# Weight columns of a dense expert pass: row one-hot times gate on ScalarE, column one-hot on VectorE in 32 bits, the PSUM copy one step later, and no products on GpSimd

## The chip, the cores and the metric

The kernel runs on one core of one Trainium2 chip. The time is the device time of one launch in microseconds (us); lower is better. Before the change it is 3195.77 us, the median of 3 runs (3186.97 to 3201.72).

## The reference, cut to what matters

An encoder block on 1024 tokens of width 1024: a mixer (attention and a short convolution, both gated), then PEER, an expert layer that this change touches. PEER chooses 16 of 128 x 128 single-neuron experts per token and head, 8 heads:

```python
q = (xc @ w_query).reshape(c, PEER_HEADS, 2, PEER_HALF_DIM)
sc = jnp.einsum('chpd,hpnd->chpn', q, sub_keys)
s1, i1 = lax.top_k(sc[:, :, 0], PEER_TOPK)
s2, i2 = lax.top_k(sc[:, :, 1], PEER_TOPK)
cand = (s1[..., :, None] + s2[..., None, :]).reshape(c, PEER_HEADS, -1)
top, pos = lax.top_k(cand, PEER_TOPK)
eidx = jnp.take_along_axis(cidx, pos, axis=-1)      # cidx = i1 * 128 + i2
g = jax.nn.softmax(top, axis=-1)
a = jax.nn.gelu(jnp.einsum('chkd,cd->chk', expert_u[eidx], xc))
out = jnp.einsum('chk,chkd->cd', g * a, expert_v[eidx])
```

## The kernel before, in words

The 1024 tokens are 8 tiles of 128. Tiles 0 to 4 (group 0) get a dense expert pass: all 16384 experts are multiplied, and a weight that is zero for experts not chosen is multiplied in. Tiles 5 to 7 (group 1) gather the rows of their chosen experts from HBM, two VectorE passes a row (L746, L755).

The stages, in the order of time: projections and mixer of group 0, its expert scores (`scores`, L556; `pq`, `pcs`), then the mixer and the scores of group 1 (lines `pc`, `px`, `pb`, `pg`, `ps`, `po`, `py`, `ph`, `pq`), then the dense pass (`z`, `pout`, `held` on TensorE, L905) with the gather of group 1 beside it, and the rest of the gather.

Two jobs run beside the scores of group 0 and the mixer of group 1. `select_gen` (L594) chooses the experts of a tile in two halves of 4 heads: top 16 of 128 by max, find and replace (L588 to L592), the same among candidates, then by one-hots the indices: `sc<-pf,iota_k` on VectorE (L637), times the index on GpSimd (L639), summed on VectorE (L640). `weights_gen` (L686) turns the chosen indices of a dense tile into columns of weights: 4 tokens (`WQ`) a step, 8 steps a block of 32 (`WT`), 4 blocks a tile, 5 tiles: 160 steps. In a step VectorE makes both one-hots in 16 bits in one instruction (`ms`, L714, 1024 elements), GpSimd multiplies the row one-hot by the gate (`o1`, L718), ScalarE copies the column one-hot into 32 bits (`o2`, L720), TensorE multiplies the two for each token (`pw`, L695), and ScalarE copies the result into `wbuf` (L696), which goes to HBM by block (`w_d`, L726). `o1` and `o2` lie token by token, so that an instruction which writes them for 4 tokens at once, token innermost, steps 512 bytes from each element to the next. `ms`, `o1` and `o2` have two buffers each, `wbuf` one.

The dense pass reads the columns back (`wt<-w_d`, L920) and multiplies them in on VectorE (`pr`, L930) ahead of the split `ph`, `phl` (L896, L898) that the second half of the dense products needs.

The jobs are generators that `tick` advances by modelled time of TensorE. Then a scheduler sets each engine's order by its own model of time; on the chip each engine goes through its own list in that order and waits where an operand is late. After the last mixer line, `drain(wgt)` (L881) runs what is left of the columns.

Of the kernel before, what the change touches and what calls it, by code (L numbers as in the profile page):

```python
# [10 lines left out]
F32 = mybir.dt.float32  # L11
BF16 = mybir.dt.bfloat16
# [3 lines left out]
AF = mybir.ActivationFunctionType  # L16
ALU = mybir.AluOpType
# [3 lines left out]
P = 128  # L21
# [29 lines left out]
WT = 32  # L51
WQ = 4
# [13 lines left out]
def block_kernel(ctx, tc, x, wqkv, wcols, wpr, wo, wq, skT, uv, uT, an_w, fn_w, fin_w, sub_w,  # L66
# [527 lines left out]
    def select_gen(small, tt, ev, gw, done=None):  # L594
# [6 lines left out]
        for a in range(2):  # L601
# [5 lines left out]
                top16(t, sc[:, hp, :], NK, sv[:, hp, :], si[:, hp, :])  # L607
                yield
            ohs = sc.rearrange("p h c -> p (h c)").bitcast(BF16).rearrange("p (j h a k) -> p j h a k", j=2, a=TOPK, k=TOPK)
            sf = t([P, PH, TOPK], F32, "sf")  # L610
            V.tensor_copy(out=sf, in_=si)
            svv = sv.rearrange("p (h q) k -> p h q k", q=2)
            sfv = sf.rearrange("p (h q) k -> p h q k", q=2)
# [11 lines left out]
            for j in range(2):  # L625
                pi, pj, pf = t(s3, U32, "pi"), t(s3, U32, "pj"), t(s3, BF16, "pf")
                if j == 0:
                    V.tensor_scalar(pi, ti, 4, None, op0=ALU.logical_shift_right)
                    V.tensor_scalar(pj, ti, 2, None, op0=ALU.logical_shift_right)
                    V.scalar_tensor_tensor(pf, pj, -12.0, pi, op0=ALU.add, op1=ALU.max)  # L630
                else:
                    V.tensor_scalar(pi, ti, 12, None, op0=ALU.bitwise_and)
                    V.tensor_scalar(pj, ti, 3, None, op0=ALU.bitwise_and)
                    V.scalar_tensor_tensor(pf, ti, 64.0, pi, op0=ALU.is_lt, op1=ALU.mult)
                    V.tensor_tensor(out=pf, in0=pf, in1=pj, op=ALU.add)
                oh = ohs[:, j]
                V.tensor_tensor(out=oh, in0=pf.unsqueeze(2).broadcast_to(sh), in1=iota_k.unsqueeze(1).broadcast_to(sh),  # L637
                                op=ALU.is_equal)
                PL.tensor_tensor(out=oh, in0=oh, in1=sfv[:, :, j, :].unsqueeze(3).broadcast_to(sh), op=ALU.mult)  # L639
                V.tensor_reduce(out=ev[j][:, a * 64:(a + 1) * 64].rearrange("p (h k) -> p h k", k=TOPK),  # L640
                                in_=oh.rearrange("p h a k -> p h k a"), axis=AX.X, op=ALU.add)
                yield
# [41 lines left out]
        yield from select_gen(t, tt, ev, gw, done)  # L684

    def weights_gen(wf):  # L686
        later = []
# [3 lines left out]
        def finish(buf, q, o1, o2):  # L691
            for t in range(0, WQ, 4):
                pw = ps["w"].tile([P, 4, NK], F32, name="pw", tag="g")
                for u in range(4):
                    PE.matmul(pw[:, u, :], lhsT=o2[:, t + u, :], rhs=o1[:, t + u, :], start=True, stop=True)  # L695
                A.copy(out=buf[:, :, q + t:q + t + 4], in_=pw.rearrange("p t i -> p i t"))  # L696

        for c in range(NB):
            while c >= len(chosen):
                yield  # L700
            pt = ps["w"].tile([P, 4, P], F32, name="ptw", tag="g")
            for j, s in enumerate(chosen[c]):
                PE.transpose(out=pt[:, j, :], in_=s, identity=ident)
            ib = wf.tile([P, 2, P], BF16, name="ib", tag="ib", bufs=2)
            A.copy(out=ib, in_=pt[:, 0:2, :])
            w = wf.tile([P, P], F32, name="wtr", tag="wtr", bufs=2)
            A.copy(out=w, in_=pt[:, 2, :])
            for b in range(P // WT):
# [116 lines left out]
    with ExitStack() as pb:  # L825
# [7 lines left out]
        with ExitStack() as st:  # L833
# [209 lines left out]
```

## Time and profile before

| | us |
|---|---|
| median of 3 runs | 3195.77 |
| the profiled execution, its own time | 3191.78 |
| span of its instructions | 3190.0 |
| busy TensorE, VectorE, ScalarE, GpSimd | 3012.1, 2646.3, 1302.9, 923.5 |
| columns: first and last `ms` starts | 732.6, 1313.4 |
| first and last product of the dense pass | 1317.7, 3147 |

Some 1.8 us of the execution lie outside the span. Busy shares of the whole span mix stages with different limits; the rows further below are therefore by stretch of time. In the stretch of the columns TensorE, VectorE, ScalarE and GpSimd all take part, and the stage ends when the last column has gone to HBM and come back.

### The profile page before, as it was taken

The page shows a single profiled execution, that of the slowest core. Times are in us where ns is not written, and L with a number is a line of the kernel's source. Part 1 is how long each engine was busy: PE and PEld are TensorE (multiplying, and loading weights), DVE is VectorE, ACT ScalarE, POOL GpSimd, SP SyncE. Part 2 cuts the span into 40 slices and gives each one's busy share as a digit, 9 for nine tenths or more (in the row PEclk, how much of TensorE's full clock was granted, in tenths as well). Part 3 has the DMA queues.
Part 4 walks back from the last instruction along what each step waited for, and adds up shares of the span by engine and source line. Part 5 has one row for each costly group of instructions (what it writes and reads, how often), then busy time and mean ns, then how long its engine had stood idle before and what let it go on. Part 6 is the DMA issues. An engine that isn't in the chain of part 4 may idle for free.

```text
span 3190.0 us, 45907 instructions
## 1 busy us (share of the span) xinstructions
PE 3012.1 (94%) x17551; PEld 2761.0 (87%) x17551; DVE 2646.3 (83%) x4665; ACT 1302.9 (41%) x2344; POOL 923.5 (29%) x716
## 2 busy tenths in 40 slices
PE   7999999898989879799999999999999999999994
PEld 6799998798988869789989989899889999999993
DVE  5442466378999996799999999999999999999898
ACT  3322364335567766533333333333333333333332
POOL 2310000035344444223222222223332323333333
PEclk9999999999999989899999999999999999999997
DMA  5451232555444375779878888888889999898887
GB/s 180 145 182 67 83 113 80 199 172 213 146 172 157 144 260 196 255 249 333 316 277 321 316 299 309 295 316 293 313 328 343 340 341 348 326 347 325 328 336 281
DMA packets 237549, 801.11 MB, mean 251 GB/s; under 512 B 18832, under 2 KB 123280, under 8 KB 174096
## 3 DMA queue, kind: packets, MB, share of 16 engines
q0 software_dynamic: 64704, 442.53, 37.5%
q1 hardware_dynamic: 152592, 305.30, 27.8%
q10 hardware_dynamic: 20032, 50.34, 4.1%
q8 instruction: 138, 2.26, 0.3%
q14 instruction: 83, 0.68, 0.1%
HBM read 714.74 MB, written 83.36 MB: 250 GB/s over the span
## 4 chain that ended last, share of the span: by engine, by line
PE 56%; DVE 17%; issue 11%; DMA 8%; POOL 4%; ACT 3%; SPq 0%; ACTq 0%; POOLq 0%; DVEq 0%
PE z L905 17%; PE pout L905 10%; PE held L905 6%; PE pq L228 4%; PE pg L228 4%; POOL uvt L739 3%; PE ph L228 3%; DMA uvt<-in_uv,idx 3%; DVE acc L755 2%; PE py L228 2%; PE pw L695 2%; DVE uvt L746 2%; DVE ms L714 1%; PE pv L228 1%; PE pk L228 1%
## 5 line engine op out<-in xcount | busy, mean ns | idle before, releaser
L739 POOL DMA_INDIRECT uvt<-in_uv,idx x384 | 528.1, 1375 | 1288.5 <-DVE acc L755 1011.0
L905 PE MATMUL z<-actTh,uh 128*128 128x320 f32 x2048 | 636.3, 311 | 5.5 <-ACT pr L929 4.5
L905 PE MATMUL z<-actTh,uhl 128*128 128x320 f32 x2048 | 636.5, 311 | 1.1 <-DVE uhl L898 1.1
L905 PE MATMUL z<-actTl,uh 128*128 128x320 f32 x2048 | 635.3, 310 | 0.0
L746 DVE SCALAR_TENSOR_TENSOR uvt<-uvt,hng 128x1024 f32<-128x1024 f32 x384 | 468.0, 1220 | 41.1 <-DMA uvt<-in_uv,idx 40.3
L755 DVE SCALAR_TENSOR_TENSOR acc<-uvt,wt,acc 128x1024 f32<-128x1024 f32 x381 | 487.8, 1280 | 1.3 <-ACT wt L749 1.2
L905 PEld LDWEIGHTS z<-actTh,uh 128*128 128x128 f32 x2048 | 386.0, 188 | 20.5 <-ACT pr L929 8.6
L905 PEld LDWEIGHTS z<-actTl,uh 128*128 128x128 f32 x2048 | 386.2, 189 | 10.1
L905 PEld LDWEIGHTS z<-actTh,uhl 128*128 128x128 f32 x2048 | 386.8, 189 | 8.5 <-DVE uhl L898 2.2
L905 PE MATMUL pout<-vh,ph 128*128 128x512 f32 x768 | 302.5, 394 | 23.2 <-ACT ph L896 15.0
L905 PE MATMUL pout<-vhl,ph 128*128 128x512 f32 x768 | 301.1, 393 | 0.0
L905 PE MATMUL pout<-vh,phl 128*128 128x512 f32 x768 | 300.5, 391 | 0.0
L718 POOL TENSOR_TENSOR o<-ms,wtr 128x512 f32<-128x512 bf16 x160 | 203.0, 1311 | 262.1 <-PE pw L695 123.4
L748 ACT ACTIVATE wt<-zt 128x1 f32<-128x1 f32 x384 | 77.0, 201 | 493.3 <-DVE uvt L746 493.0
L957 DVE TENSOR_TENSOR hacc<-pout,hacc 128x512 f32<-128x512 f32 x384 | 259.4, 681 | 19.6 <-PE pout L905 19.1
L185 DVE TENSOR_TENSOR wl<-wr,wh 128x2048 fp32r<-128x2048 f32 x66 | 157.9, 2392 | 117.7 <-ACT wh L184 117.7
L896 ACT CAST uh<-raw 128x1024 fp32r<-128x1024 f32 x128 | 134.3, 1049 | 193.5 <-DMA raw<-in_uT 187.9
L184 ACT CAST wh<-wr 128x2048 fp32r<-128x2048 f32 x74 | 141.0, 1907 | 168.9 <-DMA wr<-in_wq 31.6
L695 PE MATMUL pw<-o,o 128*128 128x128 f32 x1280 | 169.1, 284 | 41.2 <-POOL o L718 17.6
L695 PEld LDWEIGHTS pw<-o,o 128*128 128x128 f32 x1280 | 161.1, 198 | 49.3 <-issue 25.6
L905 PE MATMUL held<-vhl,ph 128*128 128x512 f32 x512 | 199.6, 391 | 0.0
L720 ACT CAST o<-ms 128x512 f32<-128x512 bf16 x160 | 179.6, 1138 | 38.8 <-DVE ms L714 26.0
(290 smaller groups left out, 6673.5 us busy)
## 6 DMA issues: line engine op xcount, KB each, us to landing
raw<-in_uT SPq DMA_DIRECT2D x128, 512.0 KB
raw<-in_uv SPq DMA_DIRECT2D x128, 512.0 KB
w_d<-wbuf ACTq DMA_DIRECT2D x20, 2048.0 KB
wt<-w_d SPq DMA_DIRECT2D x32, 1280.0 KB
wr<-in_wcols SPq DMA_DIRECT2D x28, 1024.0 KB
wr<-in_wq SPq DMA_DIRECT2D x24, 1024.0 KB
xt<-in_x SPq DMA_DIRECT2D x16, 512.0 KB
q_d<-qt POOLq DMA_DIRECT2D x32, 256.0 KB
```

The lines of the kernel that those rows point to most:

```text
L184: A.copy(out=op[0][sl], in_=src)
L185: lo.tensor_sub(op[1][sl], src, op[0][sl].bitcast(F32))
L228: PE.matmul(pd, lhsT=l[a], rhs=r[b], start=i == 0 and j == 0, stop=i == n - 1 and j == len(c) - 1)
L695: PE.matmul(pw[:, u, :], lhsT=o2[:, t + u, :], rhs=o1[:, t + u, :], start=True, stop=True)
L718: PL.tensor_tensor(out=o1.rearrange("p t i -> p i t"), in0=ms[:, 0], in1=w[:, ts].unsqueeze(1).broadcast_to(sh), op=ALU.mult)
L720: A.copy(out=o2.rearrange("p t i -> p i t"), in_=ms[:, 1])
L739: PL.indirect_dma_start(out=t[:], out_offset=None, in_=uv, in_offset=bass.IndirectOffsetOnAxis(ap=sels[c][1][:, k:k + 1], axis=0))
L746: V.scalar_tensor_tensor(u, u, 1.0, st[c], op0=ALU.mult, op1=ALU.mult, accum_out=zt)
L755: V.scalar_tensor_tensor(st["acc"], v, wt, st["acc"], op0=ALU.mult, op1=ALU.add)
L896: A.copy(out=hi, in_=t)
L905: PE.matmul(ps, lhsT=lhs[k][a], rhs=rhs[k][b], start=first and k == 0 and j == 0, stop=last and k == n - 1 and j == 2)
L957: V.tensor_add(hacc[:, t - NR, ds], ps, hacc[:, t - NR, ds])
```

## The change

The one-hot instruction of a step makes the row one-hot alone, in 16 bits (512 elements). A second VectorE instruction makes the column one-hot straight into the 32-bit `o2`, by the strided write. ScalarE makes `o1` with four instructions, one a token, each a copy scaled by the gate. The copy out of PSUM (`keep`) comes a step after its products (`columns`), and blocks and tiles are no longer drained where they end, but once at the end (`flush`), and once before the PSUM pool of the first stretch closes. In the selection the product with the index moves from GpSimd to VectorE, and the indices `sf` are kept in 16 bits.

```diff
-            sf = t([P, PH, TOPK], F32, "sf")
+            sf = t([P, PH, TOPK], BF16, "sf")
...
-                PL.tensor_tensor(out=oh, in0=oh, in1=sfv[:, :, j, :].unsqueeze(3).broadcast_to(sh), op=ALU.mult)
+                V.tensor_tensor(out=oh, in0=oh, in1=sfv[:, :, j, :].unsqueeze(3).broadcast_to(sh), op=ALU.mult)
...
+        def operands(c, b, q, ib, w):
+            ts = slice(b * WT + q, b * WT + q + WQ)
+            ms = wf.tile(sh, BF16, name="ms", tag="ms")
+            V.tensor_tensor(out=ms, in0=ib[:, 0, ts].unsqueeze(1).broadcast_to(sh), in1=iota_t, op=ALU.is_equal)
+            o2 = wf.tile([P, WQ, NK], F32, name="o2", tag="o2")
+            V.tensor_tensor(out=o2.rearrange("p t i -> p i t"), in0=ib[:, 1, ts].unsqueeze(1).broadcast_to(sh),
+                            in1=iota_t, op=ALU.is_equal)
+            o1 = wf.tile([P, WQ, NK], F32, name="o1", tag="o1")
+            for u in range(WQ):
+                A.activation(o1[:, u, :], ms[:, :, u], AF.Copy, scale=w[:, b * WT + q + u:b * WT + q + u + 1])
+            made.append((c, b, q, o1, o2))
...
                 for q in range(0, WT, WQ):
-                    ms = wf.tile([P, 2] + sh[1:], BF16, name="ms", tag="ms")
-                    V.tensor_tensor(out=ms, in0=ib[:, :, ts].unsqueeze(2).broadcast_to([P, 2] + sh[1:]),
-                                    in1=iota_t.unsqueeze(1).broadcast_to([P, 2] + sh[1:]), op=ALU.is_equal)
...
-                    PL.tensor_tensor(out=o1.rearrange("p t i -> p i t"), in0=ms[:, 0],
-                                     in1=w[:, ts].unsqueeze(1).broadcast_to(sh), op=ALU.mult)
-                    A.copy(out=o2.rearrange("p t i -> p i t"), in_=ms[:, 1])
-                    if later:
-                        finish(*later.pop(0))
-                    later.append((buf, q, o1, o2))
+                    operands(c, b, q, ib, w)
+                    if done:
+                        keep()
+                    if len(made) > 1:
+                        columns()
                     yield
-                finish(*later.pop(0))
-                A.dma_start(out=w_d[c * (P // WT) + b], in_=buf)
+            flush()
```

The scheduler then puts the work in other places. First TensorE, where the scores of group 1 end and the dense pass begins (`pq`, `pcs` are the scores, `pw` one step of columns, `z` the dense pass), before:

```order
L228 MATMUL pq_12064<-hnTh,wl 128x384
L695 MATMUL pw<-o_10523,o_10524 128x128 x4
L564 MATMUL pcs<-sk,qp 128x128 x3
L695 MATMUL pw<-o_10535,o_10536 128x128 x4
L564 MATMUL pcs<-sk,qp 128x128 x3
L695 MATMUL pw<-o_10547,o_10548 128x128 x4
L695 MATMUL pw<-o_10559,o_10560 128x128 x4
L905 MATMUL z<-actTh,uh 128x320
```

And the same place now:

```order
L228 MATMUL pq_12578<-hnTh,wl 128x384
L564 MATMUL pcs<-sk,qp 128x128 x6
L708 MATMUL pw<-o_10670,o_10668 128x128 x4
L708 MATMUL pw<-o_10720,o_10718 128x128 x4
...
L708 MATMUL pw<-o_11022,o_11020 128x128 x4
L708 MATMUL pw<-o_11037,o_11035 128x128 x4
L925 MATMUL z<-actTh,uh 128x320
```

Two steps of columns stood between the last score and the dense pass; now there are 14. Second VectorE, from the last one-hots to the first `pr` of the dense pass (`sv`, `si`, `tk` are the second half of tile 5's selection, `e` its sums, `idx` the indices of its first half), before:

```order
L714 TENSOR_TENSOR ms<-ib,iota_t 128x1024
L679 SCALAR_TENSOR_TENSOR idx<-e_12215,e_12216 128x64
L898 TENSOR_TENSOR uhl<-raw,uh 128x1024 x2
L898 TENSOR_TENSOR vhl<-raw,vh 128x1024 x2
L588 MAX sv<-sc 128x8 x6
L589 MAX_INDEX si<-sv,sc 128x8
...
L592 MAX_INDEX si<-sv,tk_12591 128x8
L930 TENSOR_TENSOR pr<-pr,wt 128x640
L590 MATCH_REPLACE tk_12597<-sv,sc 128x128
L591 MAX sv<-tk_12597 128x8
```

And now:

```order
L918 TENSOR_TENSOR vhl<-raw,vh 128x1024
L697 TENSOR_TENSOR o_10864<-ib,iota_t 128x128x4
L695 TENSOR_TENSOR ms<-ib,iota_t 128x512
...
L590 MATCH_REPLACE tk_13183<-sv,sc 128x128
L697 TENSOR_TENSOR o_11035<-ib,iota_t 128x128x4
L591 MAX sv<-tk_13183 128x8
...
L639 TENSOR_TENSOR sc<-sc,sf 128x1024
L640 TENSOR_REDUCE e_12696<-sc 128x64
L950 TENSOR_TENSOR pr<-pr,wt 128x640
```

The whole second half of tile 5's selection now stands ahead of the first `pr`, most of it ahead of the last one-hot of the columns (`o_11035`), together with five of the splits `uhl` and `vhl`.

## Rows read from the trace of the kernel before

**Rows 1.** Windows: stretch, length; busy of PE, PEld, DVE, ACT, POOL; clock; DMA; GB/s.

```profile
0.00:695.20 695.20, 655.03 (x3978) 599.57 (x3979) 338.13 (x550) 260.65 (x439) 90.26 (x112) 0.98 0.40 137
695.20:1224.10 528.90, 465.74 (x2950) 440.61 (x2950) 492.71 (x1327) 338.22 (x497) 237.64 (x172) 0.95 0.50 182
1224.10:1317.20 93.10, 91.89 (x643) 91.34 (x641) 61.02 (x149) 66.33 (x95) 39.10 (x31) 1.00 0.47 165
1317.20:1360.30 43.10, 25.25 (x144) 23.49 (x145) 24.62 (x91) 12.51 (x15) 5.76 (x5) 0.80 0.98 342
1360.30:3147.00 1786.70, 1772.73 (x9837) 1605.14 (x9836) 1697.73 (x2512) 616.18 (x1274) 536.68 (x386) 1.00 0.88 318
3147.00:3190.00 43.00, 1.46 (x7) 0.85 (x5) 32.08 (x42) 9.00 (x26) 14.08 (x12) 0.57 0.72 266
```

**Rows 2.** Waits of VectorE from 695.2 to 1224.1: total us, times, longest.

```profile
DVE sv L588 <- DMA sc<-sc_d: 9.7, 4, 5.6
DVE ms L714 <- ACT o L720: 7.3, 4, 2.9
DVE wl L185 <- ACT wh L184: 7.1, 5, 2.5
DVE ms L714 <- POOL o L718: 3.0, 3, 1.0
```

**Rows 3.** Chain of waits at the stage's end: start, length, work.

```profile
1317.69 10.34 DMA w_d<-wbuf
1328.05 19.98 DMA wt<-w_d
1348.06 0.83 DVE pr L930
```

**Rows 4.** A step's instructions: min/median/max ns; then groups: busy us, mean ns.

```profile
L714 DVE TENSOR_TENSOR ms<-ib,iota_t x160: 654/679/2030, 732.6 to 1313.4; 128x1024 bf16<-128x1024 bf16 x160
L718 POOL TENSOR_TENSOR o<-ms,wtr x160: 1056/1132/3630, 733.4 to 1314.2; 128x512 f32<-128x512 bf16 x160
L720 ACT CAST o<-ms x160: 1058/1133/1367, 733.3 to 1314.2; 128x512 f32<-128x512 bf16 x160
L696 ACT COPY wbuf<-pw x160: 563/592/765, 738.4 to 1317.0; 128x512 f32<-128x512 f32 x160
...
L714 DVE TENSOR_TENSOR ms<-ib,iota_t 128x1024 bf16<-128x1024 bf16 x160 | 128.6, 816 | 32.3 <-ACT o L720 22.6 <-POOL o L718 9.7
```

**Rows 5.** VectorE elsewhere: dense 512, strided and dense reductions of 1024; ns.

```profile
L957 DVE TENSOR_TENSOR hacc<-pout,hacc x384: 660/682/699, 1365.0 to 3153.6; 128x512 f32<-128x512 f32 x192
L640 DVE TENSOR_REDUCE e<-sc x32: 2003/2123/2265, 684.8 to 2274.4; 128x64 f32<-128x1024 bf16 x32
L387 DVE TENSOR_REDUCE nm<-ps x64: 1197/1216/1226, 354.6 to 1074.6; 128x1 f32<-128x1024 f32 x64
```

**Rows 6.** Two `ms` in a row in the chain of waits.

```profile
822.17 1.21 DVE ms L714 x2
```

**Rows 7.** Stretched VectorE instructions: min/median/max ns, and means by group.

```profile
L634 DVE SCALAR_TENSOR_TENSOR pf<-ti,pi x16: 207/460/1934, 682.0 to 2255.1; 128x64 bf16<-128x64 uint32 x16
...
L634 DVE SCALAR_TENSOR_TENSOR pf<-ti,pi 128x64 bf16<-128x64 uint32 x16 | 15.0, 940 | 0.0
...
L185 DVE TENSOR_TENSOR wl<-wr,wh x66: 2268/2291/3779, 11.4 to 1287.6; 128x2048 fp32r<-128x2048 f32 x66
...
L185 DVE TENSOR_TENSOR wl<-wr,wh 128x2048 fp32r<-128x2048 f32 x30 | 75.5, 2516 | 12.0 <-ACT wh L184 12.0
```

**Rows 8.** ScalarE, a copy of 128 elements with a per-partition scale.

```profile
L449 ACT ACTIVATE at<-po,rz x32: 349/367/493, 371.8 to 1103.3; 128x128 f32<-128x128 f32 x32
```

**Rows 9.** Waits of TensorE from 695.2 to 1317.2, those of the columns.

```profile
PE pw L695 <- POOL o L718: 17.6, 15, 3.0
PE pw L695 <- ACT o L720: 12.6, 10, 4.2
PE pw L695 <- ACT wbuf L696: 10.9, 3, 9.2
```

More of the change, by code (lines that the diff above doesn't have):

```diff
@@ L686, in weights_gen, with columns, keep, flush @@
     def weights_gen(wf):
-        later = []
         iota_t = wf.tile([P, NK, WQ], BF16, name="iota_t", tag="iota_t", bufs=1)
         repeated_iota(wf, iota_t, "wtr")
[L691 to L696, printed above, removed]
+        made, done, at = [], [], {}
+        sh = [P, NK, WQ]
+        def operands(c, b, q, ib, w):
[9 more added lines that the diff above has]
+            made.append((c, b, q, o1, o2))
+        def columns():
+            c, b, q, o1, o2 = made.pop(0)
+            pw = ps["w"].tile([P, WQ, NK], F32, name="pw", tag="g")
+            for u in range(WQ):
+                PE.matmul(pw[:, u, :], lhsT=o2[:, u, :], rhs=o1[:, u, :], start=True, stop=True)
+            done.append((c, b, q, pw))
+        def keep():
+            c, b, q, pw = done.pop(0)
+            if q == 0:
+                at["buf"] = wf.tile([P, NK, WT], F32, name="wbuf", tag="wbuf", bufs=1)
+            A.copy(out=at["buf"][:, :, q:q + WQ], in_=pw.rearrange("p t i -> p i t"))
+            if q == WT - WQ:
+                A.dma_start(out=w_d[c * (P // WT) + b], in_=at["buf"])
+        def flush():
+            while done:
+                keep()
+            while made:
+                columns()
+                keep()
+        state["flush"] = flush
         for c in range(NB):
@@ L708, in weights_gen @@
             for b in range(P // WT):
-                buf = wf.tile([P, NK, WT], F32, name="wbuf", tag="wbuf", bufs=1)
                 for q in range(0, WT, WQ):
-                    ts = slice(b * WT + q, b * WT + q + WQ)
-                    sh = [P, NK, WQ]
-                    ms = wf.tile([P, 2] + sh[1:], BF16, name="ms", tag="ms")
-                    V.tensor_tensor(out=ms, in0=ib[:, :, ts].unsqueeze(2).broadcast_to([P, 2] + sh[1:]),
-                                    in1=iota_t.unsqueeze(1).broadcast_to([P, 2] + sh[1:]), op=ALU.is_equal)
-                    o1 = wf.tile([P, WQ, NK], F32, name="o1", tag="o1")
-                    o2 = wf.tile([P, WQ, NK], F32, name="o2", tag="o2")
-                    PL.tensor_tensor(out=o1.rearrange("p t i -> p i t"), in0=ms[:, 0],
-                                     in1=w[:, ts].unsqueeze(1).broadcast_to(sh), op=ALU.mult)
-                    A.copy(out=o2.rearrange("p t i -> p i t"), in_=ms[:, 1])
-                    if later:
-                        finish(*later.pop(0))
-                    later.append((buf, q, o1, o2))
+                    operands(c, b, q, ib, w)
+                    if done:
+                        keep()
+                    if len(made) > 1:
+                        columns()
                     yield
-                finish(*later.pop(0))
-                A.dma_start(out=w_d[c * (P // WT) + b], in_=buf)
+            flush()
     def gather_gen(gat):
@@ L854, in block_kernel @@
             ready.update(range(2, NB))
+            state["flush"]()
     pa = ExitStack()
```

## The prediction, made before the changed kernel was run

> **What bounds the kernel now.** I read the windows by stage first, since the change sits in one stage. In [rows 1] the columns run from the second to the third stretch, 695.2 to 1317.2 us. In the second, VectorE is busy 492.7 of 528.9 us (93%), TensorE 465.7 (88%), ScalarE 64%, GpSimd 45%. In the third, which holds the scores of group 1, TensorE is busy 91.9 of 93.1 us and VectorE only 61.0. So VectorE sets the pace until 1224 and TensorE from there to 1317. The fourth stretch is a wait: the last block of columns goes out in 10.3 us and comes back in 20.0 us before `pr` can start [rows 3]. The dense pass that follows is TensorE's (1772.7 of 1786.7 us busy), and the last 43 us are the rest of the gather. The dense pass cannot absorb a late start: what the column stage ends later moves the end by nearly as much.
>
> Second I read the waits of VectorE in the second stretch [rows 2]. Of 36.2 us idle (528.9 - 492.7), 16.8 are waits for operands from memory or for a split (9.7 + 7.1), which stay; 10.3 are waits of `ms` for ScalarE and GpSimd to free a buffer (7.3 + 3.0). Third, the durations of a step's instructions [rows 4].
>
> **The change part by part.** All on VectorE unless said; paces are durations less the overlap with the next instruction. Two `ms` of 679 ns median took 1.21 us together [rows 4, 6], so the pace is 0.60 us, 0.07 to 0.08 below the duration.
>
> `ms` halved. 1024 elements take 654 ns at least; with about 0.12 us fixed (an estimate), half of the rest is 0.27, so 0.39 in duration and 0.33 in pace. Bounds are half the old pace, 0.30, and three quarters of it, 0.45. Saved: 160 x (0.60 - 0.33) = 43 us (24 to 48).
>
> `o2`, new. No row shows VectorE writing single 32-bit elements 512 bytes apart. From below it costs as a dense instruction of 512: 682 ns [rows 5], pace 0.61. ScalarE does this same write now, and takes 1133 ns for 512 elements where its unstrided write of 512 takes 592 [rows 4]: 0.54 us for the stride. VectorE's own nearest row is a reduction that reads single elements apart, 2123 ns for 1024 against 1216 for the dense one [rows 5]: 0.91 for 1024, 0.45 for 512. Added to 682 that is 1.13 to 1.22 us. The nearest row by kind of access is ScalarE's write, whose whole instruction takes 1133 ns with a larger fixed part. I take 1.07 us, a little under it, thus a pace of 1.0, and keep 0.61 below and 1.30 above (twice the dense row, as the stride makes ScalarE's 1.9 times its own). Added: 160 x 1.0 = 160 us (98 to 208).
>
> ScalarE's row shows that the stride costs, in this memory and at this step. [...]
>
> Products of the selection. Up to the first `pr` the 12 halves of tiles 0 to 5 are chosen, two products each: 24. [...] Added: 24 x 1.15 = 28 us (14 to 29). On GpSimd they vanish, and it waits for nothing that ends late.
>
> Stretching that ends. `ms` has a mean of 816 ns and a median of 679 [rows 4]: 160 x 0.137 = 22 us. `pf` has a mean of 940 and a least of 207 [rows 7]: 16 x 0.73 = 12. `wl` has a mean of 2516 here and a median of 2291 over the run: 30 x 0.225 = 7. These 41 us are instructions that take up to three or nine times their least while GpSimd works (237.6 + 39.1 us in both stretches, [rows 1]); almost all of GpSimd's work goes. Smaller groups do the same, so I take 60 us (41 to 80). [...]
>
> The order. The second half of tile 5's selection and five splits now stand ahead of the last `o2`, or soon behind it. Before, they were most of VectorE's 24.6 us (91 instructions) between 1317 and 1360 and some after it [rows 1]. Three quarters of that, 18 us (10 to 25), now delay the last column. What remains behind the last `o2` lies under the 30 us in which the columns go out and back [rows 3], and costs nothing; without that cover it would be some 15 us.
>
> Net on VectorE up to the last column: 160 - 43 + 28 - 60 + 18 = 103 us more.
>
> What it can use up: its idle time in the third stretch, 93.1 - 61.0 = 32 us, and 8 of the 10 us in which `ms` waited for a buffer: 40 us. The stage therefore ends 103 - 40 = 63 us later.
>
> TensorE has the same instructions. Its 14 steps in a row wait for VectorE, and that wait is the 63 us seen from the other side. ScalarE trades 160 x 1.13 = 181 us for 640 copies at about 0.37 [rows 8], 235 us: 54 more, and even with 0.1 more each for the strided read 118; it has 622 - 404.5 = 217 us free in the two stretches [rows 1], so this is hidden. In the last 14 steps, a step costs it 4 x 0.37 + 0.59 = 2.1 us, 29 us in all; VectorE needs 14 x 1.33 and the 18 us moved there, 37 us, so there too ScalarE is the lesser. The copy out of PSUM a step later frees ScalarE from waits and moves nothing. The indices in 16 bits cost nothing.
>
> In the dense pass VectorE loses the moved selection (some 20 us) and gains 8 products (9 us); TensorE's idle time there is 14 us in all [rows 1], so I put the gain at 5 us (0 to 10). The gather's tail stays.
>
> Sum, on the profiled execution's 3191.8 us: 3191.8 + 63 - 5 = 3250 us. That execution is 4 us under the median of 3195.8, which is within the spread of the three runs; so I predict 3250, 1.7% slower.
>
> **The rivals.**
>
> The strided write costs more: a pace of 1.30. The sum rises by 160 x 0.30 = 48 to 3298 us. For it: ScalarE's instruction nearly doubles by the stride. Against: the strided read adds less.
>
> The strided write is as cheap as a dense one, pace 0.61: 62 us less, net 41, which the 40 us of idle time take up. Then 3191.8 - 5 = 3187 us, no change that can be told. For it: no VectorE row shows a penalty on a write. Against: the same write on ScalarE.
>
> The other side: the hand-offs decide, not VectorE's load. TensorE waits 17.6 + 12.6 + 10.9 = 41 us for the columns' GpSimd product, ScalarE copy and PSUM copy [rows 9]; the new pipeline has no GpSimd in it and copies late. If VectorE's net stays under its 40 us of idle time, which needs `o2` at a pace of 0.60, or 0.73 with 80 us of stretching gone, TensorE gets these 41 us back, in the stretch up to 1224: 3191.8 - 41 - 5 = 3146 us. Against: VectorE is at 93% there, and TensorE's waits are late operands of a full VectorE at one remove.
>
> That the change does not do what it says is excluded: `o1` and the products are in the order as ScalarE's and VectorE's instructions.
>
> **How the numbers follow.** The forecast gets 0.57, with a range of its own of 3215 to 3280 (the ends of the stretching, and 0.1 us in the pace of `o2`). The dearer write gets 0.12, the dense write 0.17, the hand-offs 0.14. About 0.5% (16 us) is what a measurement of this kernel can tell from no change. Slower by more: 0.57 + 0.12 = 0.69. Faster by more: the hand-offs and a little of the dense write, 0.15. Within it: 0.16. The range from 3180 to 3310 holds the forecast, nearly all of the dense write and more than half of the dearer one, some 0.8.
>
> **What would show it.** In the profile after: a median of `o2` near 1.07 us (0.68 and 1.4 are the two rivals); `ms` near 0.39; the products near 1.2; means of `ms`, `pf`, `wl` close to their medians; VectorE busy over 93% up to the last column, the third stretch included; the last column near 1380 instead of 1317, with `pr` some 40 us behind it; and TensorE waiting for `o2` in its 14 steps. If the last column is at 1317 or before, or if VectorE has idle time left there, the forecast's mechanism is wrong; if it is late but ScalarE's four copies end the waits, the place was wrong.

## The result, and the profile after

The changed kernel takes 3234.62 us (median of 4 runs, 3230.24 to 3239.42), beside 3198.74 us for the kernel before (4 runs): a ratio of 1.0123, with a 95% interval from 1.010 to 1.0146. It is slower, by 36 us or 1.2%. The profiled execution of after took 3239.42 us, that of before 3191.78; this pair stands 47.6 us apart, some 12 us more than the medians, so differences between two traces are read below with that much doubt. Two of all the runs behind this document had a clearly lower granted clock and are left out of the ratios: one of e11 (4264.94 us at 0.652) and one of the kernel before beside e1 to e4 (3283.28 us at 0.874).

The windows by stage of after, in the columns of [rows 1] (the third line runs to the first `z`, the fourth to the first `pr`, the last from the last `pr` to the end):

```profile
695.20:1224.10 528.90, 443.34 (x2738) 416.45 (x2737) 498.66 (x1367) 335.75 (x808) 37.02 (x22) 0.93 0.46 167
1224.10:1317.20 93.10, 89.73 (x608) 88.82 (x607) 77.60 (x208) 67.37 (x164) 0.00 (x0) 0.99 0.50 178
1317.20:1377.90 60.70, 42.42 (x246) 38.79 (x244) 57.75 (x175) 40.36 (x105) 0.00 (x0) 0.78 0.46 164
1377.90:1393.40 15.50, 12.49 (x72) 12.23 (x73) 14.10 (x42) 3.29 (x4) 4.69 (x4) 0.89 0.79 272
1393.40:3170.10 1776.70, 1766.29 (x9831) 1607.30 (x9830) 1665.66 (x2458) 608.66 (x1261) 510.50 (x370) 1.00 0.88 320
3170.10:3237.60 67.50, 21.43 (x85) 16.45 (x83) 54.99 (x74) 15.15 (x44) 22.95 (x18) 0.69 0.76 272
```

In the second stretch VectorE goes from 492.7 to 498.7 us and TensorE falls from 465.7 to 443.3; in the third VectorE rises from 61.0 to 77.6; then follows a new stretch of 60.7 us, in which VectorE is busy 57.8 and TensorE 42.4. The columns end there, 60 us later than before. The same stretch from 695.2 us to the first `z`, before (first line) and after:

```profile
695.20:1317.70 622.50, 557.64 (x3591) 531.97 (x3590) 554.09 (x1475) 404.99 (x592) 276.75 (x202) 0.96 0.50 179
```

```profile
695.20:1377.90 682.70, 575.49 (x3588) 544.06 (x3586) 634.00 (x1748) 443.48 (x1075) 37.02 (x22) 0.93 0.47 168
```

VectorE does 79.9 us more (634.0 against 554.1) and idles 19.7 us less (48.7 against 68.4): together the 60.2 us by which the first `z` is later.

A step's instructions after, to be read beside [rows 4] and [rows 8] (min/median/max ns), with the selection's product and the `pf` of [rows 7]:

```profile
L695 DVE TENSOR_TENSOR ms<-ib,iota_t x160: 387/416/3048, 741.7 to 1373.5; 128x512 bf16<-128x512 bf16 x160
L697 DVE TENSOR_TENSOR o<-ib,iota_t x160: 1008/1071/1127, 742.0 to 1374.6; 128x512 f32<-128x512 bf16 x160
L701 ACT ACTIVATE o<-ms,wtr x640: 388/400/465, 742.1 to 1375.1; 128x128 f32<-128x128 bf16 x160
L715 ACT COPY wbuf<-pw x160: 559/572/627, 748.3 to 1377.2; 128x512 f32<-128x512 f32 x160
L639 DVE TENSOR_TENSOR sc<-sc,sf x32: 1191/1218/1255, 681.3 to 2307.7; 128x1024 bf16<-128x1024 bf16 x32
L634 DVE SCALAR_TENSOR_TENSOR pf<-ti,pi x16: 205/217/4517, 682.4 to 2290.4; 128x64 bf16<-128x64 uint32 x16
```

What TensorE waits for from 695.2 to the first `z` (us, times, longest), where [rows 9] had GpSimd's and ScalarE's operands:

```profile
PE pw L708 <- DVE o L697: 40.0, 25, 5.7
PE pw L708 <- ACT wbuf L715: 19.7, 13, 6.4
```

The chain at the end of the columns (start, length, work), to set beside [rows 3]: VectorE's list, selection and one-hots in turn, runs without a gap up to the last one-hot, and only then ScalarE and TensorE finish the last step.

```profile
1371.29 0.85 DVE o L697
1372.13 0.28 DVE tk L590
1372.42 0.02 issue
1372.44 0.29 DVE sv L591
1372.73 0.95 DVE o L697
1373.68 0.25 DVE ms L695
1373.93 0.28 DVE si L592
1374.21 0.00 issue
1374.21 1.31 ACT o L701 x4
...
1376.05 1.17 PE pw L708 x8
1377.22 0.02 issue
1377.24 0.59 ACT wbuf L715
```

Note the lengths of `o2` in this chain, 0.85 and 0.95 us, beside its duration of 1.07: the next instruction starts some 0.1 to 0.2 us before this one has ended.

Four points of time split every run: the first `z`, the first `pr`, the last `pr`, the end. The rows of `pr`, before (first) and after, with its first and last start:

```profile
L930 DVE TENSOR_TENSOR pr<-pr,wt x128: 787/817/2573, 1348.1 to 3127.4; 128x640 f32<-128x640 f32 x128
```

```profile
L950 DVE TENSOR_TENSOR pr<-pr,wt x128: 793/818/851, 1393.4 to 3170.1; 128x640 f32<-128x640 f32 x128
```

The same four points for all the experiments below, from the same rows of each profiled execution (us; VectorE's busy time is counted from 695.2 us; "columns" is the time from the first `z` to the first `pr`, in which the last block goes out and comes back; "rest" is from the last `pr` to the end):

| kernel | VectorE busy to first `z` | first `z` | columns | dense | rest | span |
|---|---|---|---|---|---|---|
| before | 554.1 | 1317.7 | 30.4 | 1779.3 | 62.6 | 3190.0 |
| after | 634.0 | 1377.9 | 15.5 | 1776.7 | 67.5 | 3237.6 |
| e1, o2 dense | 589.5 | 1344.0 | 16.0 | 1775.1 | 65.3 | 3200.4 |
| e2, strided read | 598.4 | 1428.3 | 15.2 | 1776.9 | 67.2 | 3287.6 |
| e3, product on GpSimd | 639.1 | 1394.9 | 14.7 | 1785.9 | 46.5 | 3242.0 |
| e4, o1 on GpSimd | 691.5 | 1424.5 | 27.6 | 1766.1 | 54.0 | 3272.2 |
| e5, o2 by token | 588.7 | 1340.5 | 15.4 | 1774.9 | 66.9 | 3197.7 |
| e6, before + product | 583.6 | 1345.8 | 15.8 | 1774.7 | 59.0 | 3195.3 |
| e7, copy in its step | 631.6 | 1378.1 | 15.5 | 1774.7 | 65.7 | 3234.0 |
| e8, both on ScalarE | 553.8 | 1383.7 | 17.7 | 1782.6 | 40.8 | 3224.8 |
| e9, e5 + selection | 574.7 | 1333.3 | 15.7 | 1773.8 | 57.3 | 3180.1 |
| e10, e9, o2 shared | 573.1 | 1344.3 | 14.9 | 1776.6 | 40.8 | 3176.6 |
| e11, e6 + selection | 552.6 | 1323.3 | 24.2 | 1779.6 | 70.3 | 3197.4 |

### The profile page after: what moved, and what is told of

Read it like the earlier page. It is cut to its first block, busy times and chain, and to the rows that moved or that the text cites. A ratio compares the mean times of both kernels' runs of the same rounds, so it can differ in the third digit from the quotient of the medians.

```text
span 3237.6 us, 46201 instructions
## 1 busy us (share of the span) xinstructions
PE 3028.0 (94%) x17551; PEld 2776.2 (86%) x17551; DVE 2708.3 (84%) x4857; ACT 1331.2 (41%) x2822; POOL 661.4 (20%) x524
## 4 chain that ended last, share of the span: by engine, by line
PE 44%; issue 19%; DVE 19%; DMA 9%; POOL 6%; ACT 2%; SPq 0%; POOLq 0%; ACTq 0%; DVEq 0%
PE z L925 13%; PE pout L925 7%; POOL uvt L758 6%; PE held L925 5%; PE pg L228 4%; PE pq L228 3%; DMA uvt<-in_uv,idx 3%; DVE o L697 3%; PE py L228 2%; PE ph L228 2%; DVE wl L185 2%; DVE acc L774 1%; PE pv L228 1%; PE pk L228 1%; DMA raw<-in_uT 1%
## 5 line engine op out<-in xcount | busy, mean ns | idle before, releaser
L925 PEld LDWEIGHTS z<-actTh,uh 128*128 128x128 f32 x2048 | 388.0, 189 | 22.8 <-ACT pr L949 11.2
L708 PE MATMUL pw<-o,o 128*128 128x128 f32 x1280 | 188.7, 299 | 69.0 <-DVE o L697 40.0
L708 PEld LDWEIGHTS pw<-o,o 128*128 128x128 f32 x1280 | 176.0, 210 | 83.7 <-issue 30.1
L185 DVE TENSOR_TENSOR wl<-wr,wh 128x2048 fp32r<-128x2048 f32 x66 | 150.9, 2287 | 115.5 <-ACT wh L184 115.5
L701 ACT ACTIVATE o<-ms,wtr 128x128 f32<-128x128 bf16 x640 | 209.0, 404 | 82.5 <-DVE ms L695 43.6
L949 ACT ACTIVATE pr<-z 128x640 f32<-128x640 f32 x128 | 90.2, 705 | 339.0 <-PE z L925 319.9
L184 ACT CAST wh<-wr 128x2048 fp32r<-128x2048 f32 x74 | 140.9, 1906 | 169.2 <-DMA wr<-in_wq 29.8
```

What stands on the lines that cost most here:

```text
L184: A.copy(out=op[0][sl], in_=src)
L185: lo.tensor_sub(op[1][sl], src, op[0][sl].bitcast(F32))
L701: A.activation(o1[:, u, :], ms[:, :, u], AF.Copy, scale=w[:, b * WT + q + u:b * WT + q + u + 1])
L708: PE.matmul(pw[:, u, :], lhsT=o2[:, u, :], rhs=o1[:, u, :], start=True, stop=True)
L925: PE.matmul(ps, lhsT=lhs[k][a], rhs=rhs[k][b], start=first and k == 0 and j == 0, stop=last and k == n - 1 and j == 2)
```

## The experiments

**e1: the price of the stride alone.** The same instruction on the same tiles, written densely; its ones lie in other places of `o2`, so the columns are not those of the reference. The order on every engine is that of after.

```diff
-            V.tensor_tensor(out=o2.rearrange("p t i -> p i t"), in0=...
+            V.tensor_tensor(out=o2.rearrange("p t i -> p (t i)").rearrange("p (i t) -> p i t", t=WQ), in0=...
```

> The column one-hot is written to o2 densely (token innermost, no 512-byte steps), while TensorE still reads o2 as before, so the columns hold misplaced ones: the output is not the reference's. The order on every engine is that of the changed kernel. Theory (VectorE's load sets the end of the column stage, and the strided write is its largest new part): L697 falls from 1071 to about 680 ns, VectorE loses 160 x 0.39 = 62 us, the last column comes about 50 us earlier (1325 instead of 1374), time about 3185 us (3175 to 3200). Rival (ScalarE's four copies and the PSUM copy set the pace, TensorE waits for them): the time stays above 3225 although L697 is shorter.

3203.07 us (10 runs), ratio to before 1.0021 (1.0002 to 1.004). The instruction's row in e1:

```profile
L697 DVE TENSOR_TENSOR o<-ib,iota_t x160: 665/685/710, 742.7 to 1340.4; 128x512 f32<-128x512 bf16 x160
```

The stride costs 1071 - 685 = 386 ns, 62 us in 160 steps by duration. VectorE's busy time up to the first `z` falls by 44.5 us (0.28 a step), the first `z` comes 33.9 earlier, and the time falls by 31.5. So VectorE's work decides the end of the stage in the changed kernel, and the strided write is most of the loss of 36 us. The size that I expected was too large (3175 to 3200 us): of the 62 us I put 50 into time. One reason is in e1's own trace: in the last 20 us ahead of the first `z` its chain no longer runs through VectorE, but from the write of the block before, which holds the one `wbuf`, through ScalarE's copies (for these writes they wait 15.3 us in e1 and 15.1 in e5):

```profile
1322.28 9.68 DMA w_d<-wbuf
```

With the stride gone, VectorE does not decide alone. The rival, over 3225, falls.

**e2: the stride moved to TensorE's read.** `o2` is kept token innermost, written densely, and TensorE reads its weights 16 bytes apart.

```diff
-            o2 = wf.tile([P, WQ, NK], F32, name="o2", tag="o2")
+            o2 = wf.tile([P, NK, WQ], F32, name="o2", tag="o2")
...
-                PE.matmul(pw[:, u, :], lhsT=o2[:, u, :], rhs=o1[:, u, :], start=True, stop=True)
+                PE.matmul(pw[:, u, :], lhsT=o2[:, :, u], rhs=o1[:, u, :], start=True, stop=True)
```

> The same dense write, and TensorE loads the column one-hots with a step of 16 bytes, so that the columns are right again. Theory: as with the dense write alone, about 3185 us (3175 to 3200), if a weight load takes 190 ns with this step too. If the step doubles the load to 380 ns, it is longer than the product of 275 ns and 1280 of them cost up to 1280 x 0.1 = 130 us of TensorE: above 3235 us. Rival (ScalarE sets the pace): above 3225 with loads unchanged.

3288.93 us (4 runs), ratio 1.0287 (1.027 to 1.0304): the worst of all. Weight loads and products of the columns in e2, then in after:

```profile
L708 PEld LDWEIGHTS pw<-o,o x1280: 307/329/333, 742.8 to 1427.1; 128*128 128x128 f32 x183
L708 PE MATMUL pw<-o,o x1280: 270/397/603, 742.8 to 1427.2; 128*128 128x128 f32 x183
```

```profile
L708 PEld LDWEIGHTS pw<-o,o x1280: 186/192/338, 743.1 to 1376.8; 128*128 128x128 f32 x183
L708 PE MATMUL pw<-o,o x1280: 270/275/583, 743.2 to 1376.9; 128*128 128x128 f32 x183
```

The load takes 137 ns more and the product behind it 397 - 275 = 122 ns more, 156 us in 1280; the case that I had named, a dearer load and a time above 3235, came. TensorE is busy 692.1 of the 733.1 us up to the first `z` (575.5 of 682.7 in after), so the limit is TensorE's here. Handing the stride to TensorE costs more than it saves.

**e3: the selection's product back on GpSimd.**

```diff
-                V.tensor_tensor(out=oh, in0=oh, in1=sfv[:, :, j, :].unsqueeze(3).broadcast_to(sh), op=ALU.mult)
+                PL.tensor_tensor(out=oh, in0=oh, in1=sfv[:, :, j, :].unsqueeze(3).broadcast_to(sh), op=ALU.mult)
```

> The product with the index in the selection goes back to GpSimd, everything else as changed. Theory: VectorE loses 24 x 1.15 = 28 us before the last column and gets some stretching back (GpSimd works 24 x 1.9 = 46 us there): 15 to 25 us faster than changed, about 3215 us (3205 to 3225). Rival (the change in VectorE's load does not matter): within 5 us of the changed kernel, 3230 to 3240.

3235.04 us (4 runs), ratio 1.0117 (1.01 to 1.0134): no change from after, a miss: the number is the rival's. VectorE was to be relieved of the product, but its busy time to the first `z` is 639.1 us, 5 more than after. Groups of e3 from 695.2 us to the first `z` (busy us, mean ns), then of after:

```profile
L697 DVE TENSOR_TENSOR o<-ib,iota_t 128x512 f32<-128x512 bf16 x160 | 176.4, 1112 | 11.9 <-PE pw L708 11.8
...
L634 DVE SCALAR_TENSOR_TENSOR pf<-ti,pi 128x64 bf16<-128x64 uint32 x11 | 15.5, 1409 | 0.0
```

```profile
L697 DVE TENSOR_TENSOR o<-ib,iota_t 128x512 f32<-128x512 bf16 x160 | 169.5, 1068 | 7.4 <-PE pw L708 7.2
...
L639 DVE TENSOR_TENSOR sc<-sc,sf 128x1024 bf16<-128x1024 bf16 x20 | 24.4, 1222 | 0.1
...
L634 DVE SCALAR_TENSOR_TENSOR pf<-ti,pi 128x64 bf16<-128x64 uint32 x10 | 6.5, 648 | 0.0
```

24.4 us of products leave, and 7 us return in a stretched `o2` and 9 in `pf`. The rest is the order: e3 has 20 steps of columns in a row ahead of the dense pass instead of 14, VectorE is busy only 63.8 of the 93.1 us from 1224 to 1317 (12.8 of its idle time is one wait for scores from memory, and 9.9 are waits for a buffer of `o2`), and more of the selection stands ahead of the first `z`. The rest after the last `pr` is then 21 us shorter. The run does not separate these; the product's own price comes from e6. So the rival's reason, that VectorE's load does not matter, is not shown either: the load did not fall.

**e4: the gate's product back on GpSimd.**

```diff
-            for u in range(WQ):
-                A.activation(o1[:, u, :], ms[:, :, u], AF.Copy, scale=w[:, b * WT + q + u:b * WT + q + u + 1])
+            PL.tensor_tensor(out=o1.rearrange("p t i -> p i t"), in0=ms, in1=w[:, ts].unsqueeze(1).broadcast_to(sh), op=ALU.mult)
```

> The row one-hot times gate goes back to GpSimd in one instruction of 512 elements, instead of ScalarE's four; the rest as changed. Theory (VectorE's load): stretching by GpSimd comes back (41 to 60 us), VectorE has no less to do: 20 to 45 us slower than changed, 3255 to 3280 us, with means of ms, pf and wl above their medians again. Rival (ScalarE sets the pace): ScalarE is freed of 209 us and the time falls to 3200 us or below.

3274.88 us (4 runs), ratio 1.0245 (1.0227 to 1.0262), as the theory expected. VectorE's own instructions grow, from 695 us to the end of the columns in e4:

```profile
L697 DVE TENSOR_TENSOR o<-ib,iota_t 128x512 f32<-128x512 bf16 x160 | 183.3, 1159 | 0.7 <-PE pw L707 0.6
L695 DVE TENSOR_TENSOR ms<-ib,iota_t 128x512 bf16<-128x512 bf16 x160 | 82.4, 525 | 0.0
```

In after the means are 1068 and 432 ns: 184 ns a step, 29 us. VectorE is busy 57.5 us more up to the first `z`, and 40 us of it reach the end; some half of the 57.5 is these 29 us, and the rest is not taken apart. The order differs here too (20 steps in a row). Taking GpSimd out of the steps is a gain of the change, as the forecast's stretching term had it. A few instructions carry it: the median of `o2` is 1064 ns and that of `ms` 414 (1071 and 416 in after), but single ones take up to 1906 and 4534 (1127 and 3048 in after). What lengthens the single ones is not shown; shown are medians that stay and means that are together 184 ns a step higher.

**e5: the same `o2`, each element in its place, without the stride.** Each token's 128 columns are written in a row; the token's index is read as a constant, the list of numbers from a tile of its own.

```diff
+        iota_r = wf.tile([P, NK], BF16, name="iota_r", tag="iota_r", bufs=1)
+        V.tensor_copy(out=iota_r, in_=iota_t[:, :, 0])
...
-            V.tensor_tensor(out=o2.rearrange("p t i -> p i t"), in0=ib[:, 1, ts].unsqueeze(1).broadcast_to(sh),
-                            in1=iota_t, op=ALU.is_equal)
+            V.tensor_tensor(out=o2, in0=ib[:, 1, ts].unsqueeze(2).broadcast_to([P, WQ, NK]),
+                            in1=iota_r.unsqueeze(1).broadcast_to([P, WQ, NK]), op=ALU.is_equal)
```

> VectorE makes the column one-hot token by token (element innermost), so that it is written densely in the layout that TensorE loads; the rest as changed. Theory (the 512-byte step of the write was the dear part, and the dense write took 31 us off): L697 about 690 ns and the time that of the dense write, about 3203 us (3190 to 3215). Rival (reading one 2-byte index again and again costs as much as the step did): L697 stays near 1070 ns and the time near 3235 us.

3202.52 us (12 runs), ratio 1.0021 (1.0009 to 1.0033), with `o2` at a median of 684 ns: e1's time, now with the ones where the products want them.

**e6: the kernel before with the selection's product alone on VectorE** (`sf` in 16 bits, as in the change).

```diff
-                PL.tensor_tensor(out=oh, in0=oh, in1=sfv[:, :, j, :].unsqueeze(3).broadcast_to(sh), op=ALU.mult)
+                V.tensor_tensor(out=oh, in0=oh, in1=sfv[:, :, j, :].unsqueeze(3).broadcast_to(sh), op=ALU.mult)
```

> The kernel before with the selection's product alone moved to VectorE and the indices in 16 bits. Theory (VectorE's load): 22 to 24 products of 1.15 us less 5 to 10 us of stretching by GpSimd, and some of VectorE's idle time taken up: 5 to 20 us slower than before, 3203 to 3218 us. Rival (the product costs nothing on either engine, as its return to GpSimd moved the changed kernel by nothing): 3192 to 3202 us.

3198.23 us (12 runs), ratio 1.0008 (0.9995 to 1.002): nothing, a miss by the time, which is the rival's. But the table shows the price that was expected: VectorE's busy time to the first `z` rises by 29.5 us and the first `z` is 28.1 later. It is given back: 14.6 us by the shorter way of the columns, 4.6 in the dense pass, 3.6 in the rest. (These are differences of single profiled executions; the two spans stand 5.3 us apart.) So "nothing at the end" is not "nothing in the stage".

**e7: the copy out of PSUM in its own step.**

```diff
-                    if done:
-                        keep()
...
+                        keep()
```

> The changed kernel with the copy out of PSUM in the same step as its products again, instead of a step later. Theory: ScalarE has time to spare, so nothing moves: 3225 to 3245 us. Rival (the later copy is what keeps ScalarE's queue from blocking, and TensorE waits for ScalarE's one-hots): 10 to 30 us slower, 3245 to 3265 us.

3233.7 us (4 runs), ratio 1.0111 (1.0091 to 1.0132): as after, as expected. The later copy moves nothing (the order differs a little: 12 steps in a row instead of 14).

**e8: both operands on ScalarE.** VectorE makes both one-hots in 16 bits as before; ScalarE copies `o2` (dense write) and scales `o1`; the selection's one-hots are laid out so that its product and sum read in a row.

```diff
...
+            V.tensor_tensor(out=ms2, in0=ib[:, :, ts].unsqueeze(2).broadcast_to([P, 2] + sh[1:]),
+                            in1=iota_t.unsqueeze(1).broadcast_to([P, 2] + sh[1:]), op=ALU.is_equal)
...
+            A.copy(out=o2, in_=ms2[:, 1].rearrange("p i t -> p t i"))
...
+                V.tensor_tensor(out=oh, in0=pf.unsqueeze(3).broadcast_to(sh), in1=iota_k.unsqueeze(1).broadcast_to(sh),
...
+                V.tensor_tensor(out=oh, in0=oh, in1=sfv[:, :, j, :].unsqueeze(2).broadcast_to(sh), op=ALU.mult)
...
+                                in_=oh, axis=AX.X, op=ALU.add)
```

> VectorE makes both one-hots in one 16-bit instruction again, ScalarE copies the column one-hot into 32 bits with a dense write and a strided read (about 0.6 us instead of the 1.13 of the strided write), GpSimd stays out, and the selection's one-hots lie so that its product and its sum read densely (product 0.68 instead of 1.22 us, sum 1.2 instead of 2.1, one-hot 1.2 instead of 0.68). Theory (VectorE's load): VectorE has 160 x 0.73 + 24 x 0.9 = 138 us less than in the changed kernel up to the last column, ScalarE 160 x 0.55 = 88 us more, which it has free: 50 to 75 us faster than changed, 3160 to 3185 us. Rival (ScalarE then sets the pace, at 2.4 us a step, and 22 steps stand in a row ahead of the dense pass): 3210 us or more.

3225.8 us (4 runs), ratio 1.0085 (1.0064 to 1.0107): the theory's 3160 to 3185 is missed, and the time is the rival's. VectorE is back at 553.8 us, the figure of before, and yet the first `z` is 66 us later. What TensorE waits for up to the first `z` in e8, and ScalarE's two kinds of copy:

```profile
PE pw L711 <- ACT wbuf L718: 83.3, 43, 13.1
```

```profile
L701 ACT CAST o<-ms x160: 629/661/742, 740.9 to 1378.5; 128x512 f32<-128x512 bf16 x160
L704 ACT ACTIVATE o<-ms,wtr x640: 388/403/490, 741.5 to 1380.0; 128x128 f32<-128x128 bf16 x160
```

A step costs ScalarE 0.66 + 4 x 0.40 + 0.58 = 2.8 us, and its other work of the stage comes on top: it is busy 528.5 of 688.5 us, and the PSUM copy behind it in its list ends TensorE's waits. VectorE waits too: 46.3 us for ScalarE to free `ms`, 36.5 for ScalarE's half of a split and 27.3 for scores from memory. So ScalarE, busy for 77% of the stretch, is in most of the waits; but 22 steps stand in a row here, and the end of the chain runs through VectorE's selection again. That the limit is ScalarE alone is not shown; shown is that VectorE's busy time alone no longer tells the end of the stage.

**e9: e5 with the selection laid out as in e8.** The edit is that of `pf`, `sfv` and the sum in e8's diff, on e5.

> The kernel after with o2 written densely token by token, and the selection's one-hots laid out so that the reduction and the product read 16-bit elements in a row. In e8_scalar_columns that product took 685 ns and that reduction 1212 where after has 1218 and 2073, the compare 1219 instead of some 680: 0.86 us saved for each of 22 products, 19 us of VectorE. 6 steps of columns stand in a row ahead of the dense pass, where e5_tokens has 14. Theory (VectorE's load sets the end of the stage, and some half of it reaches the end): 3202.5 - 10 = 3192 us, a ratio of 0.997 to 1.000 to before. Rival 1 (the selection's instructions lie in VectorE's gaps and reach the end by nothing, as e3_sel_gpsimd and e6_sel_vector suggest): 3199 to 3206, ratio 1.001 to 1.003. Rival 2 (the 14 steps in a row are what is left of the cost, and 6 are cheap): below 3188.

3193.28 us (12 runs), ratio 0.998 (0.9966 to 0.9994), close to the theory's 3192. In the order 14 steps stand in a row, not 6 as the expectation has it, so rival 2 was not tested. Product and sum in e9 are

```profile
L641 DVE TENSOR_TENSOR sc<-sc,sf x32: 657/684/693, 681.7 to 2229.2; 128x1024 bf16<-128x1024 bf16 x32
L642 DVE TENSOR_REDUCE e<-sc x32: 1187/1210/1222, 687.7 to 2233.7; 128x64 f32<-128x1024 bf16 x32
```

where after has 1218 ns for the product. VectorE's busy time to the first `z` falls by 14 us against e5, and the first `z` comes 7.2 earlier.

**e10: in one step of four ScalarE makes `o2`.**

```diff
+            own = q // WQ % 4 == 3
...
+            if own:
+                A.copy(out=o2, in_=mw[:, 1].rearrange("p i t -> p t i"))
```

> As e9_tokens_sel, and in one step of four ScalarE makes o2 as a copy from the second half of ms, so that VectorE saves some 0.39 us in 40 steps (16 us) and ScalarE spends 0.67 us more in each of them (27 us). Theory (VectorE's load): half of 16 below e9_tokens_sel, 3184 us, or 6 to 12 below it. Rival (ScalarE is near its own bound, as in e8_scalar_columns): at or above e9_tokens_sel, 3192 to 3210.

3179.72 us (6 runs), ratio 0.9948 (0.9927 to 0.9968): faster than before by 0.5%, and the fastest of all. The number is within the expectation; the reason is not. VectorE is busy 573.1 us up to the first `z`, as in e9, and the first `z` is 11 us later: TensorE's waits for the PSUM copy are 37.1 us instead of e9's 20.6, which is the rival's direction, and 18 steps stand in a row instead of 14. The gain stands in the rest after the last `pr`: 40.8 us. VectorE's passes over gathered rows in that stretch, first after, then e10:

```profile
L774 DVE SCALAR_TENSOR_TENSOR acc<-uvt,wt,acc 128x1024 f32<-128x1024 f32 x16 | 20.4, 1278 | 0.7 <-ACT wt L768 0.6
```

```profile
L785 DVE SCALAR_TENSOR_TENSOR acc<-uvt,wt,acc 128x1024 f32<-128x1024 f32 x7 | 8.9, 1276 | 0.0
```

16 rows are left for the end in after, 13 in e9, 7 in e10 (and 9 and 8 in e3 and e8, whose rest is short too), and each costs two passes of 1.2 to 1.3 us. How many are left follows from VectorE's list, in which rows and dense work take turns; no run changed that alone. (The profiled execution of e9 is the fastest of its 12, 11 us under their median, so the split between e9 and e10 is read from unequal runs.)

**e11: e6 with the same selection.** The edit is that of e9 on e6; the columns are those of before.

> The kernel before, with the selection's product on VectorE in 16 bits and its one-hots laid out as in e9_tokens_sel; the columns are untouched (ms of both one-hots, o1 on GpSimd, o2 on ScalarE). VectorE's load falls by 19 us against e6_sel_vector (3198 us). Theory (half of it reaches the end): 3188 us, ratio 0.995 to 0.999. Rival (selection lies in gaps): 3196 to 3201, ratio 0.999 to 1.002.

3199.17 us (12 runs, those in the ratio from 3179.99 to 3216.16), ratio 1.0002 (0.9978 to 1.0025): no change, the rival's time. VectorE's busy time to the first `z` does fall, by 31 us against e6, and the first `z` comes 22.5 earlier; but the columns' way is 24.2 us instead of 15.8, the dense pass 4.9 longer and the rest 11.3. The stage answered as the theory said, and the end did not. The rival's reason, that the selection lies in gaps, is not what the trace shows.

## Why the prediction was right

It was right in sign and in what it put first, VectorE's load and the strided write, and near in size: 3250 forecast, 3234.6 measured, and the forecast's own range of 3215 to 3280 held it. Some of the nearness is luck: two terms were too large and cancelled, and one was missing. Point by point:

- **VectorE decides the stage.** Shown for the changed kernel by e1, where every engine keeps its order and only a VectorE instruction gets shorter. Against before, the first `z` is later by 60.2 us for 79.9 us more of VectorE's work (after), 26.3 for 35.4 (e1), 22.8 for 34.6 (e5), 28.1 for 29.5 (e6), 77.2 for 85.0 (e3), 106.8 for 137.4 (e4), 60.4 for 77.5 (e7), 15.6 for 20.6 (e9): 0.66 to 0.95 of it. It fails where another engine enters: e2 (TensorE) and e8 (waits for ScalarE). The changes in e10 and e11 are too small or too mixed to tell.
- **The strided write.** 1.07 us forecast, 1071 ns measured; the dense one 685. Its pace was mis-sized: I took 1.0, the durations less 0.07, while the chain of after shows 0.85 to 1.0 and e1 puts the whole difference to a dense write (0.60 in its chain) at 0.28. Counted in the trace of after from each start to VectorE's next, the 160 of them take 145.7 us, so the term of 160 is 146. One row was misread: ScalarE's copy of 592 ns, which the forecast called unstrided, writes runs of four elements 128 bytes apart and reads PSUM in hops of 512 bytes, so 0.54 us was not the price of the stride alone; the upper bound of 1.30 leaned on it, the value taken less. Of the 1071 ns for 512 elements, an estimated 1.86 ns is for each once the 0.12 us are taken off that the forecast counted as fixed; the least durations of `ms`, 654 ns for 1024 elements [rows 4] and 387 for 512, leave the same 0.12. ScalarE's fixed part, which the forecast called larger, is by the same reckoning an estimated 0.32 us (e8, across two kinds of copy: 403 ns for 128 elements, 661 for 512). No run has VectorE write these elements at another step, so the price is that of 512 bytes alone.
- **`ms` halved, the products.** 416 ns, 0.25 to 0.33 in the chain (0.33 forecast). By the same count `ms` falls from 119.5 to 56.2 us, 63; 19 of that is its stretching (below), 44 the halving (43 forecast). Products 1.22 us each, 20 of them between 695.2 us and the first `z` in after, two ahead of that and two behind: 24 us by duration, 23 by the count (28 forecast). The 1.15 us a product in the forecast's sum was the author's estimate; no run shows it, and the 1.22 us stand in its place.
- **Stretching and order.** The mean of `ms` over its median went from 137 to 16 ns (19 us). VectorE's other instructions that are equally many before and after in this stretch get 43 us shorter by the same count: `wl` from a mean of 2516 to 2284 ns, `dv` from 999 to 206, and smaller ones (one `pf` of 4517 ns is left). Together that is 62 us, 60 forecast. Those that are more in after, the moved selection and the splits, add 18 us, and 18 were forecast. The sum by the count is 146 - 44 + 23 - 62 + 18 = 81 us, beside 79.9 by busy time and 103 forecast: the difference is the pace of `o2` and the number of products. That the stretching ends because GpSimd is out of the steps is borne out by e4, where it comes back (184 ns a step).
- **Idle time to use up.** The term that failed most: 40 us forecast, 19.7 found. In the third stretch VectorE rose to 77.6 of 93.1 us, not to the full: TensorE is the full engine there (89.7 us), and VectorE's idle 15.5 us are waits, 5.4 of them `o2` for a buffer that `pw` frees and 4.5 scores from memory. What the forecast took for free time was in part time in which VectorE had nothing to work on. Together with the smaller sum, 103 - 40 = 63 became 80 - 20 = 60; two misses cancelled. The forecast had also asked for VectorE over 93% busy up to the last column, the third stretch included, and had named idle time left there as a sign that its mechanism is wrong. VectorE was 83% busy in the third stretch and 95% (57.8 of 60.7 us) in the new one behind it. Taken strictly, that sign speaks against the forecast; e1 shows that it was set too hard.
- **The way of the columns.** Forecast to stay near 30 us (`pr` 40 behind the last column); it is 15.5, and this is the term that the forecast lacks. It had said that the dense pass cannot absorb a late start; of the 60.2 us, 47.6 reach the end of the profiled pair and 36 the medians. In before, that stretch moves 372 GB/s, in after 272:

```profile
1317.70:1348.10 30.40, 14.68 (x96) 14.16 (x96) 12.48 (x41) 8.27 (x8) 4.82 (x4) 0.81 1.02 372
```

The rows of expert weights are called for by SyncE's queue; its issues at this place, before, then after:

```profile
1317.58 0.33 SPq L913 DMA_DIRECT2D raw<-in_uv  x1
1319.08 0.33 SPq L603 DMA_DIRECT2D sc<-sc_d  x1
1320.03 0.86 SPq L913 DMA_DIRECT2D raw<-in_uT  x1
1321.37 0.71 SPq L913 DMA_DIRECT2D raw<-in_uv  x1
1326.58 0.33 SPq L913 DMA_DIRECT2D raw<-in_uT  x1
1328.05 0.38 SPq L920 DMA_DIRECT2D wt<-w_d  x1
```

```profile
1363.66 0.33 SPq L933 DMA_DIRECT2D raw<-in_uv  x1
1384.65 0.38 SPq L940 DMA_DIRECT2D wt<-w_d  x1
```

In before, four loads of 512 KB (one of them of scores) go out in the 10 us ahead of `wt`, and the DMA engines are busy throughout the stretch (a share of 1.02 by the row above, 0.79 in after); in after the last of them is 21 us ahead, where such a load took 7.6 us in the chain of waits. These loads are not the whole reason. The way, cut where `wt` is issued, beside the bytes of gathered rows that GpSimd's queue moves while `wt` comes back:

| kernel | block out, us | `wt` back, us | gathered, MB | 512 KB loads in the 10 us ahead of `wt` |
|---|---|---|---|---|
| before | 10.4 | 20.0 | 4.19 | 3 of weights, the last 1.5 us ahead, 1 of scores |
| after | 6.8 | 8.7 | 0.71 | none |
| e4 | 7.2 | 20.4 | 4.14 | 1 of scores, 0.4 us ahead |
| e6 | 7.5 | 8.3 | 0.61 | 1 of weights, 6.4 us ahead |
| e11 | 9.3 | 14.9 | 2.90 | 2 of weights, the last 3.0 us ahead |

Most of the difference is in the way back. e4 has the longest, and its last load of expert weights went out 40 us ahead. In the first 8.7 us of the way back every one of them moves under 1 MB of gathered rows; in before and e4 another 3.3 and 3.5 MB pass while `wt` is still coming. So the traces read like this: a load just ahead delays `wt` past some 9 us, and then it shares the DMA engines with the gathered rows (in before's way back its queue takes 52.2% of their time, that of the rows 51.7%). That is a reading; no run held the loads or the rows back with all else the same.

- **Dense pass and rest.** -5 forecast for the dense pass, -2.6 found; the rest, forecast to stay, +4.9. On the profiled pair, 3191.8 + 60.2 - 14.9 - 2.6 + 4.9 = 3239.4, the time of the profiled execution of after.
- **The rivals.** The dense-cost write falls by the duration (1071 ns, 685 in e1). The dearer write falls too (1.4 us would have been its duration). The hand-offs' condition, a VectorE sum under 40 us, was not met (80): TensorE waits 40.0 us for `o2` and 19.7 for the PSUM copy, and e7, which takes the late copy away, moves nothing. ScalarE's copies at 400 ns instead of 367 are not among TensorE's waits above, so they stayed hidden, as forecast; e1 and e8 show how near ScalarE was.

## What to carry to other kernels

When an element's place costs more than its arithmetic, ask which engine pays for the step, and write densely by turning the operands instead: e5 gives the change's own result for 387 ns less a step (684 for 1071). Count what a stage loses on its deciding engine, but follow the time past the stage: here a transfer and the number of rows left for the end took or gave some 15 to 20 us, more than several of the edits were worth. And when a version wins, read where it won before you believe the reason: e10 beats e9 in its last 40 us, not by its columns.

## What the runs showed of the hardware that was not expected

- A VectorE write of 512 32-bit elements 512 bytes apart took 1071 ns (after), a dense one 685 (e1); from its start to the next on VectorE it cost 0.91 us on the mean in after, 0.61 in e1 (0.58 to 0.69 in e1's chain).
- On ScalarE the same 512 elements, 16-bit into 32-bit, took 1133 ns read in a row and written 512 bytes apart [rows 4], and 661 read 8 bytes apart and written in a row (e8).
- A weight load whose 32-bit elements lie 16 bytes apart took 329 ns instead of 192, and the product behind it 397 instead of 275 (e2).
- A VectorE product of 1024 16-bit elements took 1218 ns where one operand repeats an element along the innermost run, 684 where both run on (e9); the sum of 1024 16-bit elements took 1210 ns read in a row (e9), 2137 read 32 bytes apart (median of L640 in after).
